# Expert features in three groups instead of six, with longer weight rows and small jobs between the products

## The chip, the cores and the metric

One core of one Trainium2 chip runs the whole program. The metric is device time in microseconds of one execution; before the change the median of three runs is 2388.02 us. Profiled executions come from the hardware profiler of the same core.

## What is computed

Two transformer blocks of depth 2 on 256 tokens of 1024 features, all in float32: the first with gated feed-forwards and a mixer, the second with a mixer per layer, a dense gated feed-forward in layer 0 and a mixture of experts in layer 1. The change touches the mixture of experts alone:

```python
def swiglu_2(h, w1, w3, w2):
    return (jax.nn.silu(h @ w1) * (h @ w3)) @ w2

def moe_swiglu(h, router_w, w1, w3, w2):
    logits = (h @ router_w).astype(jnp.float32)
    top_v, top_i = lax.top_k(logits, TOP_K)            # 2 of 8 experts
    ...
    for e in range(N_EXPERTS):
        y = y + gates[..., e:e + 1] * swiglu_2(h, w1[e], w3[e], w2[e])
    return y
```

Each expert has w1 and w3 of 1024 x 2816 and w2 of 2816 x 1024, 34.6 MB together; all eight are read, 277 MB.

## The kernel before

Every product is made exact in float32 from three products of a rounded type: a matrix is written as a high part (fp32r) plus a low part. For weights, `weights` (from L136) loads 1 MB into one of five buffers `raw` (the load is issued by SP, L143), then in two parts of 128 x 1024 elements ScalarE (ACT) makes the high part `whi` (L154) and VectorE (DVE) the low part `wlo` (L156). The pools `whi` and `wlo` hold eight parts each. `mm3` (L173 to L175) issues the three products of one operand pair: token high part with `whi`, token high part with `wlo`, token low part with `whi`. With 512 columns in each product a part of 128 x 1024 feeds six products.

The mixture of experts is the function `experts`. For each expert, at most 128 of its tokens are gathered (L1230, once for two experts), and the 2816 features are worked off in six groups: five of 512 and one of 256.

- Up products: x w1 and x w3 of a group go to a PSUM tile each (`mm`). Of 512 columns of w1 or w3, half the rows (512 rows, in DRAM runs of 2 KB) come with one load; the last group loads 1024 rows of 256 columns (runs of 1 KB).
- `hid`: ACT computes silu of the first (L1351), DVE multiplies it by the second (L1352).
- `flip` (L1261): TensorE (PE) transposes the group's `hid` in blocks of 128 into PSUM; ACT copies it as a high part (L179), DVE subtracts for the low part (L180).
- `down`: products with w2 (loads of 256 rows of 4 KB), added up in two PSUM tiles `acc` over all of the expert's groups.

In the program text these are a pipeline of three steps: after a group's up products come the `down` of two groups ago and the `flip` of one group ago. At an expert's end `scatter` splits the two output tiles, and the next expert's first group is followed by `add`, all of it at once: four products that put the slots back to their tokens (L1310) and four gated additions on DVE (L1315). The last expert's output meets the gate row first (L1291, L1307).

The order of instructions on each engine is set by a scheduler when the program is built; engines then run their own list in order, and wait where an input is missing. So where a waiting instruction stands in the list decides what stands behind it.

```python
                hid = self.s2([128, 512])[:, :n]
                nc.scalar.activation(hid, ps[0], AF.Silu)
                nc.vector.tensor_mul(hid, hid, ps[1])
                if stage2:
                    down(*stage2)
                stage2 = flip(*stage1) if stage1 else None
                stage1 = (e, f0, n, hid)
```

PSUM has four `mm` and four `acc` tiles of one bank each. A second round for experts with more than 128 tokens stands in a conditional block and is not run with these inputs.

Of the kernel before, what the change touches and what calls it, by code (L numbers as in the profile page):

```python
# [17 lines left out]
F32 = mybir.dt.float32  # L18
# [17 lines left out]
# parts of the first expert that are loaded to memory that later experts' tokens take: first feature, weights, half  # L36
EARLY = ((1024, "moe_w3_2", 1), (1536, "moe_w3_2", 1), (2048, "moe_w3_2", 1))
# [7 lines left out]
class Split:  # L45
    """A float32 matrix as the exact sum of two float32r parts, row block by row block."""
# [10 lines left out]
class Features:  # L57
    """x^T of both token tiles as the exact sum of two float32r parts; tiles [128, 2 token tiles, 4 blocks, 128]."""
# [14 lines left out]
class Kernel:  # L73
# [45 lines left out]
    def spare(self, src, nparts=2):  # L119
        """src: DRAM access [128, A, B]; loaded to 4 KB slots, in parts along A"""  # L120
# [7 lines left out]
    def behind(self):  # L128
        """Queues splits of weights behind an instruction of self.order = (instruction, splits that need not wait)"""
        if not self.order:  # L130
            return nullcontext()
        ins, free = self.order
        self.order = (ins, free - 1)
        return nullcontext() if free > 0 else self.tc.issue_after(ins)

    def weights(self, src, nparts=2, xs=None):  # L136
        """src: DRAM access [128, A, B]; its exact split, in parts along A. xs: the parts, if they are loaded already."""
# [8 lines left out]
        for x in xs:  # L146
# [3 lines left out]
            # in smaller steps where other work should find its place between them  # L150
# [9 lines left out]
    def columns(self, w, c0, n, k0=0, k1=None):  # L160
        """columns c0..c0+n of a [K, N] matrix as [128, K/128, n]"""
# [31 lines left out]
    def split_features(self, part, k0, k1, src):  # L193
        """src [128, k1 - k0, 256 tokens] -> blocks k0..k1 of a part"""
# [4 lines left out]
    def transpose_tile(self, X, t, x):  # L199
        """x: [128 tokens, features] of token tile t -> its part of X"""  # L200
# [14 lines left out]
    def feat(self, w, c0, X, n=512):  # L215
        """(x w)^T for n columns of w from c0: psum tiles [128 features, 2 blocks, 256 tokens]"""
# [56 lines left out]
    def rstd(self, ms, eps, n=1):  # L273
        """(ms + eps) ** -0.5 for [128, n]"""
# [8 lines left out]
    def constants(self):  # L283
# [16 lines left out]
        # 1 for the rows of the modulation that hold scale, 8..15 and 32..39  # L300
# [12 lines left out]
        # masks of the pairs (s, t): s on partitions, t along the free axis  # L313
# [22 lines left out]
        # vectors of parameters, one column per 128 of them  # L336
# [14 lines left out]
        # silu(c)  # L351
# [3 lines left out]
        # lower bounds of the first block's gates  # L355
# [19 lines left out]
        # 8 softplus(-lambda): max(-lam, 0) + log1p(exp(-|lam|)), the logarithm as 2 atanh(e / (2 + e))  # L375
# [25 lines left out]
    def plan_ada(self):  # L401
# [4 lines left out]
        for l in range(DEPTH):  # L406
# [4 lines left out]
            # what is loaded is used some time later  # L411
# [33 lines left out]
    def ada_load(self, l, st):  # L445
        """c w as rows [48, 128]; b, and b + 1 for scale; norm gain for scale, 1 elsewhere"""
# [9 lines left out]
    def ada_rows(self, l, st):  # L456
        """c w + b with norm gain * (1 + scale) in place of scale, to DRAM, to be read by every partition"""
# [11 lines left out]
    def hidden(self, pa, pb, out):  # L469
        """silu(pa) * pb -> out (float32)"""  # L470
# [4 lines left out]
    def ffn(self, X, w1, w3, w2, finish, ahead=None):  # L475
        """(silu(x w1) * (x w3)) w2; finish(t, psum halves of [128 tokens, 512]) once token tile t is complete"""
# [33 lines left out]
        # the first 512 features one token tile after the other, so that they can start on the first tile alone  # L510
# [60 lines left out]
    def head_out(self, o, gate):  # L571
        """o: psum [128 tokens, 512] of four heads -> rms-normalised per head, times gate [128, 512]"""
# [15 lines left out]
    def mixer1(self, l, X, finish):  # L588
# [23 lines left out]
        # the scores advance by one level with every tile of weights from here on  # L612
# [21 lines left out]
        # second branch, gated  # L634
# [49 lines left out]
    def project(self, Y, w, finish, order=((0,), (1,), (2, 3))):  # L684
        """Y w in steps of 256 rows of w, of which the last of the order go tile by tile"""
# [13 lines left out]
    def cumulate(self, lf, n):  # L699
        """running sums of lf [128, n * 64] within chunks of 64"""  # L700
# [27 lines left out]
    def hgrn_scores(self, qT, kT, lf):  # L728
        """sum_k q[t,k] exp(b[t,k] - b[s,k]) k[s,k] for s <= t. Pairs in the two halves of a block of 2n tokens take
# [791 lines left out]
```

## Time and profile before

| | |
|---|---|
| runs | 2388.02 us median of 3 (2386.01 to 2391.89) |
| profiled execution, first to last instruction (its span) | 2385.1 us; its own time is not listed apart from the span |
| PE busy | 2338.5 us, 98% |
| PE weight loads busy | 2073.4 us, 87% |
| DVE busy | 1849.2 us, 78% |
| ACT busy | 1421.7 us, 60% |
| mixture of experts | from about 1577 us to the end |
| DMA in the mixture of experts, 1600 to 2368 us | 342 GB/s |

How to read it: a matmul's end is modelled by the profiler and matmuls overlap, so that the busy time of PE says little of how much room it has; starts of matmuls are recorded, and the step from one start to the next shows a wait. The span lies 2.9 us under the median of the runs.

### The profile page before, as it was taken

To read this page: it belongs to the slowest core of one execution; us is meant where nothing else is said; L and a number is where in the kernel's file an instruction comes from. 1 tells how busy PE (TensorE), PEld (TensorE's weight loads), DVE (VectorE), ACT (ScalarE), POOL (GpSimd) and SP (SyncE) were. 2 spreads that over 40 slices of the span, in tenths; PEclk is the share of its full clock that TensorE was granted. 3 is DMA by queue.
4 is the path that set the end of the run, shared out by engine and by line. 5 is a ranking of instruction groups with operands and counts; after the bars stand their busy time and mean duration, and the time that the engine had idled before them with its cause. 6 is when DMAs were issued, how large, how long until landed. Compare 5 with 4: busy or idle time off the path is not lost.

```text
span 2385.1 us, 36351 instructions
## 1 busy us (share of the span) xinstructions
PE 2338.5 (98%) x14424; PEld 2073.4 (87%) x14424; DVE 1849.2 (78%) x2465; ACT 1421.7 (60%) x1960; POOL 64.2 (3%) x102
## 2 busy tenths in 40 slices
PE   8999999999999999999999999999999999999998
PEld 8998999999999999999788998878888887888876
DVE  6877877777786886764777556789988898898897
ACT  5444754454544664454475444778877777777775
POOL 0000000000000000000100001000000000000000
PEclk9999999999999999999999999999999999999999
DMA  8886446776788455575536555378999999999995
GB/s 284 300 326 205 141 163 201 261 259 232 265 311 289 152 168 185 193 246 189 182 108 221 184 188 198 107 280 321 356 337 334 350 345 343 357 338 353 367 346 215
DMA packets 277122, 608.07 MB, mean 255 GB/s; under 512 B 12976, under 2 KB 61630, under 8 KB 276944
## 3 DMA queue, kind: packets, MB, share of 16 engines
q1 hardware_dynamic: 269776, 590.52, 70.3%
q10 hardware_dynamic: 5696, 14.34, 2.0%
q8 instruction: 115, 1.88, 0.3%
q0 software_dynamic: 1472, 0.81, 0.1%
q14 instruction: 63, 0.52, 0.1%
HBM read 604.48 MB, written 1.15 MB: 254 GB/s over the span
## 4 chain that ended last, share of the span: by engine, by line
PE 89%; DVE 6%; ACT 2%; issue 2%; DMA 0%; POOL 0%; SPq 0%; POOLq 0%; ACTq 0%; DVEq 0%
PE mm L174 19%; PE mm L173 19%; PE mm L175 19%; PE acc L174 9%; PE acc L175 8%; PE acc L173 8%; DVE wlo L156 3%; ACT whi L154 1%; PE acc L775 1%; PE mm L1261 1%; PE mm L205 1%; PE mm L1230 1%; DVE s L180 0%; PE mm L1310 0%; PE mm L961 0%
## 5 line engine op out<-in xcount | busy, mean ns | idle before, releaser
L156 DVE TENSOR_TENSOR wlo<-raw,whi 128x1024 fp32r<-128x1024 f32 (+1 forms) x1302 | 1228.2, 986 | 349.3 <-ACT whi L154 344.8
L154 ACT ACTIVATE whi<-raw 128x1024 fp32r<-128x1024 f32 (+1 forms) x1302 | 1056.3, 865 | 549.3 <-PE mm L174 195.6
L173 PE MATMUL mm<-s,whi 128*128 128x256 f32 x2224 | 630.4, 284 | 2.6 <-ACT s L179 2.4
L175 PE MATMUL mm<-s,wlo 128*128 128x256 f32 x2224 | 629.3, 283 | 0.0
L174 PE MATMUL mm<-s,whi 128*128 128x256 f32 x2224 | 629.1, 283 | 0.0
L173 PEld LDWEIGHTS mm<-s,whi 128*128 128x128 f32 x2224 | 424.8, 191 | 6.5 <-ACT s L179 2.9
L174 PEld LDWEIGHTS mm<-s,whi 128*128 128x128 f32 x2224 | 425.1, 191 | 1.7
L175 PEld LDWEIGHTS mm<-s,wlo 128*128 128x128 f32 x2224 | 425.1, 191 | 0.5
L174 PE MATMUL mm<-wlo,s 128*128 128x512 f32 (+1 forms) x1184 | 421.7, 357 | 3.0 <-DVE wlo L156 2.2
L173 PE MATMUL mm<-whi,s 128*128 128x512 f32 (+1 forms) x1184 | 419.4, 354 | 3.5 <-ACT s L179 3.2
L175 PE MATMUL mm<-whi,s 128*128 128x512 f32 (+1 forms) x1184 | 415.4, 352 | 0.8 <-DVE s L180 0.8
L174 PE MATMUL acc<-wlo,s 128*128 128x512 f32 x984 | 387.9, 395 | 1.5
L175 PE MATMUL acc<-whi,s 128*128 128x512 f32 x984 | 383.4, 392 | 0.0
L173 PE MATMUL acc<-whi,s 128*128 128x512 f32 x984 | 376.7, 393 | 5.4 <-ACT s L179 5.4
L174 PEld LDWEIGHTS mm<-wlo,s 128*128 128x128 f32 x1184 | 226.0, 191 | 41.4 <-DVE wlo L156 13.7
L173 PEld LDWEIGHTS mm<-whi,s 128*128 128x128 f32 x1184 | 226.1, 191 | 35.5 <-ACT s L179 5.8
L175 PEld LDWEIGHTS mm<-whi,s 128*128 128x128 f32 x1184 | 225.6, 191 | 29.7 <-DVE s L180 1.8
L174 PEld LDWEIGHTS acc<-wlo,s 128*128 128x128 f32 x984 | 185.6, 189 | 46.4 <-DVE wlo L156 9.8
L173 PEld LDWEIGHTS acc<-whi,s 128*128 128x128 f32 x984 | 185.5, 189 | 44.4 <-ACT s L179 7.3
L175 PEld LDWEIGHTS acc<-whi,s 128*128 128x128 f32 x984 | 185.6, 189 | 38.7 <-DVE s L180 0.5
L179 ACT ACTIVATE s<-mm 128x512 fp32r<-128x512 f32 (+1 forms) x112 | 58.5, 540 | 90.8 <-PE mm L1261 55.7
L431 DVE SCALAR_TENSOR_TENSOR s<-raw,cact,s 128x1024 f32<-128x1024 f32 x84 | 107.3, 1278 | 0.6 <-DMA raw<-in_ada_w_dram 0.2
(308 smaller groups left out, 1374.8 us busy)
## 6 DMA issues: line engine op xcount, KB each, us to landing
raw<-in_moe_w_dram SPq DMA_DIRECT2D x261, 1024.0 KB, 6.1
raw<-in_ffn_w_dram SPq DMA_DIRECT2D x164, 1024.0 KB, 5.5
raw<-in_w_in_dram SPq DMA_DIRECT2D x60, 1024.0 KB, 5.2
raw<-in_ada_w_dram SPq DMA_DIRECT2D x48, 1024.0 KB, 7.0
raw<-in_w_out_dram SPq DMA_DIRECT2D x16, 1024.0 KB, 5.0
s<-rows ACTq DMA_DIRECT2D x10, 512.0 KB, 5.0
raw<-in_w_branch_b_dram SPq DMA_DIRECT2D x4, 1024.0 KB
raw<-in_w_branch_a_dram SPq DMA_DIRECT2D x4, 1024.0 KB
```

The lines of the kernel that those rows point to most:

```text
L154: nc.scalar.activation(h[:, c], x[:, c], AF.Copy)
L156: nc.vector.tensor_sub(l[:, c], x[:, c], h.bitcast(F32)[:, c])
L173: nc.tensor.matmul(out, lh, rh, start=start, stop=False, skip_group_check=skip)
L174: nc.tensor.matmul(out, lh, rl, start=False, stop=False, skip_group_check=skip)
L175: nc.tensor.matmul(out, ll, rh, start=False, stop=stop, skip_group_check=skip)
L179: nc.scalar.activation(h, src, AF.Copy)
L205: nc.tensor.transpose(p[:, j, :], x[:, (4 * q + j) * 128:(4 * q + j + 1) * 128], self.ident)
L431: nc.vector.scalar_tensor_tensor(acc, r[:, j, :], c, acc, op0=OP.mult, op1=OP.add)
L775: nc.tensor.matmul(p[:, h], d[:, h, c], q, start=True, stop=True)
L1230: nc.tensor.matmul(p[:, j, :], part[:, k * 128:(k + 1) * 128], S[ep][:, t], start=n == 0, stop=n == 3)
L1261: nc.tensor.transpose(p[:, j, :], hid[:, j * 128:(j + 1) * 128], self.ident)
```

## The change

Groups are now 1024, 1024 and 768 features. A load of w1 or w3 takes 256 rows of a group's whole width (runs of 4 KB, or 3 KB in the last group: 768 KB per load); a load of w2 takes for each partition two neighbouring rows, one run of 8 KB, and `flip` therefore transposes every second column of `hid`. A group has two PSUM tiles per weight matrix, of 512 and 512 (or 256) columns, and two `hid` tiles, with two silus in a row and two multiplications in a row. `flip`, gather, `back` and `add` use PSUM tiles of `acc` instead of `mm`. The pipeline has two steps: `down` of a group follows the up products of the next one, and its two flips stand between these products; gather steps, additions, output splits and `back` become jobs of which one is taken after every 256 rows of an up product. Three loads for the first expert that are made early change their shape in the same way. The rest of the diff drops comments, and gives the second round 16 buffers instead of 10.

```diff
-EARLY = ((1024, "moe_w3_2", 1), (1536, "moe_w3_2", 1), (2048, "moe_w3_2", 1))
+EARLY = ((1024, "moe_w3_2", 1), (1024, "moe_w3_2", 3), (2048, "moe_w3_2", 1))
+GROUPS = ((0, 1024), (1024, 1024), (2048, 768))
...
-        groups = [(i * 512, 512) for i in range(5)] + [(2560, 256)]
-        def flip(e, f0, n, hid):
-            nb = n // 128
-            p = self.mm([128, 4, 128])
+        def flip(hid, i, to):
+            nb = hid[i].shape[1] // 128
+            v = hid[i].rearrange("p (b m j) -> p b j m", j=2, m=128)
+            p = self.acc([128, 4, 128])
             for j in range(nb):
-                nc.tensor.transpose(p[:, j, :], hid[:, j * 128:(j + 1) * 128], self.ident)
+                nc.tensor.transpose(p[:, j, :], v[:, j // 2, j % 2, :], self.ident)
...
             for r0 in range(0, n, 256):
-                W = self.wrows(a["moe_w2_2"][0][e], f0 + r0)
-                for hf in range(2):
-                    for j in range(2):
-                        b = r0 // 128 + j
+                w = a["moe_w2_2"][0][e][f0 + r0:f0 + r0 + 256, :]
+                W = self.weights(w.rearrange("(p k) f -> p k f", k=2))
+                h, l = hl[r0 // 512]
+                for j in range(2):
+                    b = r0 % 512 // 128 + j
+                    for hf in range(2):
                         self.mm3(out[e][hf], (h[:, b, :], l[:, b, :]), W(j, hf * 512, (hf + 1) * 512),
...
-                for name in ("moe_w1_2", "moe_w3_2"):
-                    w = a[name][0][e]
-                    p = self.mm([128, 512])[:, :n]
...
-                hid = self.s2([128, 512])[:, :n]
-                nc.scalar.activation(hid, ps[0], AF.Silu)
-                nc.vector.tensor_mul(hid, hid, ps[1])
-                if stage2:
-                    down(*stage2)
-                stage2 = flip(*stage1) if stage1 else None
-                stage1 = (e, f0, n, hid)
+                widths = ((0, 512), (512, n - 512))
+                flips, to = [], {}
+                if prev:
+                    flips = [lambda i=i, hid=prev[3], to=to: flip(hid, i, to) for i in range(len(prev[3]))]
+                hid = []
+                for name in ("moe_w1_2", "moe_w3_2"):
+                    ps = [self.mm([128, 512])[:, :m] for _, m in widths]
+                    for kq in range(4):
+                        W = self.wcols(a[name][0][e], f0, n, kq * 256, kq * 256 + 256, ahead.get((e, f0, name, kq)))
+                        for k in range(2):
+                            for p, (b, m) in zip(ps, widths):
+                                self.mm3(p, X(2 * kq + k, c0, c0 + 128), W(k, b, b + m), kq + k == 0,
+                                         kq == 3 and k == 1)
+                        if flips and (hid or kq == 3):
+                            flips.pop(0)()
+                        else:
+                            step()
+                    if not hid:
+                        for p, (b, m) in zip(ps, widths):
+                            hid.append(self.s2([128, 512])[:, :m])
+                            nc.scalar.activation(hid[-1], p, AF.Silu)
+                    else:
+                        for h, p in zip(hid, ps):
+                            nc.vector.tensor_mul(h, h, p)
+                if prev:
+                    down(*prev[:3], to)
+                prev = e, f0, n, hid
```

Up to the first gather of the mixture of experts the lists of all engines are the same before and after; the number of products stays the same throughout. From there on the lists differ. Three places, as the program is built:

DVE at the end of a group's up products, before the change; L1352 is the multiplication that ends `hid`, `wlo_19822` and `wlo_19826` are the two low parts of the first load of w2 behind it.

```order
L156 TENSOR_TENSOR wlo_19801<-raw_19794,whi_19800 128x1024
L156 TENSOR_TENSOR wlo_19822<-raw_19819,whi_19821 128x1024
L1352 TENSOR_TENSOR s2_19816<-s2_19816,mm_19771 128x512
L156 TENSOR_TENSOR wlo_19826<-raw_19819,whi_19825 128x1024
L156 TENSOR_TENSOR wlo_19844<-raw_19841,whi_19843 128x1024
```

DVE at the end of an expert's first group, after the change; L1384 are the two multiplications, `wlo_19124` and `wlo_19128` the two low parts of the first load of w2.

```order
L158 TENSOR_TENSOR wlo_19100<-raw_19097,whi_19099 128x1024
L158 TENSOR_TENSOR wlo_19104<-raw_19097,whi_19103 128x1024
L1384 TENSOR_TENSOR s2_19004<-s2_19004,mm_19008 128x512
L1384 TENSOR_TENSOR s2_19006<-s2_19006,mm_19009 128x512
L158 TENSOR_TENSOR wlo_19124<-raw_19121,whi_19123 128x1024
L158 TENSOR_TENSOR wlo_19128<-raw_19121,whi_19127 128x1024
```

Before, one low part of w2 stands ahead of one multiplication; now none stands ahead of two.

PE at the same end before the change, from the last three products of the up tile (`mm_19771`) to the first product that takes the low part behind the multiplication (`wlo_19826`).

```order
L173 MATMUL mm_19771<-whi_19800,s4_18954 128x512
L174 MATMUL mm_19771<-wlo_19801,s4_18954 128x512
L175 MATMUL mm_19771<-whi_19800,s4_18955 128x512
L173 MATMUL acc_19211<-whi_19821,s2_19722 128x512
L173 MATMUL acc_19212<-whi_19821,s2_19722 128x512
L174 MATMUL acc_19211<-wlo_19822,s2_19722 128x512
L175 MATMUL acc_19211<-whi_19821,s2_19723 128x512
L173 MATMUL acc_19211<-whi_19825,s2_19722 128x512
L174 MATMUL acc_19212<-wlo_19822,s2_19722 128x512
L175 MATMUL acc_19212<-whi_19821,s2_19723 128x512
L173 MATMUL acc_19212<-whi_19825,s2_19722 128x512
L174 MATMUL acc_19211<-wlo_19826,s2_19722 128x512
```

PE at the end of the first group after the change; `mm_19008` and `mm_19009` are the two up tiles.

```order
L176 MATMUL mm_19008<-wlo_19104,s4_17033 128x512
L177 MATMUL mm_19008<-whi_19103,s4_17034 128x512
L176 MATMUL mm_19009<-wlo_19104,s4_17033 128x512
L177 MATMUL mm_19009<-whi_19103,s4_17034 128x512
L175 MATMUL acc_18472<-whi_19123,s2_19000 128x512
L175 MATMUL acc_18473<-whi_19123,s2_19000 128x512
L176 MATMUL acc_18472<-wlo_19124,s2_19000 128x512
L177 MATMUL acc_18472<-whi_19123,s2_19001 128x512
```

Eight products stood between the last up product and the first one that takes a low part from behind the multiplication. Now two products of the down step do, or four counted from the end of the first up tile.

PE at the end of an expert's second group after the change; L1267 are the transposes of the two `hid` tiles that the multiplications have just ended.

```order
L177 MATMUL mm_18363<-whi_18454,s4_17034 128x512
L176 MATMUL mm_18364<-wlo_18455,s4_17033 128x512
L177 MATMUL mm_18364<-whi_18454,s4_17034 128x512
L175 MATMUL acc_18472<-whi_18476,s2_18355 128x512
L175 MATMUL acc_18473<-whi_18476,s2_18355 128x512
L1267 MATMUL acc_18652<-ident_80,s2_18359 128x128 x4
L1267 MATMUL acc_18689<-ident_80,s2_18361 128x128 x4
L176 MATMUL acc_18472<-wlo_18477,s2_18355 128x512
```

The flips that the program text puts between the next group's products stand here right behind the group itself, ahead of the low products of w2.

## Rows read from the trace of the kernel before

**Rows 1.** The page: span, then busy time, share and instructions by engine.
```profile
span 2385.1 us, 36351 instructions
PE 2338.5 (98%) x14424; PEld 2073.4 (87%) x14424; DVE 1849.2 (78%) x2465; ACT 1421.7 (60%) x1960; POOL 64.2 (3%) x102
```
**Rows 2.** Stretches: PE, PEld, DVE, ACT, POOL busy (instructions), clock, DMA share, GB/s.
```profile
1600.00:1700.00 100.00, 100.00 (x483) 83.99 (x482) 92.95 (x104) 82.48 (x90) 0.00 (x0) 1.00 0.95 340
1700.00:1800.00 100.00, 100.00 (x489) 84.33 (x488) 87.30 (x87) 76.16 (x92) 0.00 (x0) 1.00 0.95 342
...
2200.00:2300.00 100.00, 99.31 (x459) 79.76 (x458) 88.78 (x87) 71.53 (x83) 0.00 (x0) 1.00 1.00 364
```
**Rows 3.** Waits, 1560 to 2385 us: us in total, times, longest.
```profile
DVE s L1352 <- PE mm L175: 20.5, 32, 1.5
...
PEld mm L174 <- DVE wlo L156: 13.7, 32, 1.0
...
PEld acc L174 <- DVE wlo L156: 9.8, 22, 0.5
...
ACT whi L154 <- DMA raw<-in_moe_w_dram: 4.2, 6, 1.0
```
**Rows 4.** Timeline at the end of one group: start, us, engine, line [idle before].
```profile
2192.38 0.39 PE L174 MATMUL mm<-wlo,s 128*128 128x512 f32 x1
...
2192.60 0.39 PE L175 MATMUL mm<-whi,s 128*128 128x512 f32 x1
...
2193.03 0.69 DVE L1352 TENSOR_TENSOR s<-s,mm 128x512 f32<-128x512 f32 x1 [0.86 <-PE mm L175]
...
2193.63 3.49 DVE L156 TENSOR_TENSOR wlo<-raw,whi 128x1024 fp32r<-128x1024 f32 x3
...
2194.41 0.39 PE L173 MATMUL acc<-whi,s 128*128 128x512 f32 x1
...
2194.91 0.50 PE L174 MATMUL acc<-wlo,s 128*128 128x512 f32 x1
...
2195.24 0.39 PE L175 MATMUL acc<-whi,s 128*128 128x512 f32 x1
2195.25 0.19 PEld L174 LDWEIGHTS acc<-wlo,s 128*128 128x128 f32 x1
2195.47 0.40 PE L174 MATMUL acc<-wlo,s 128*128 128x512 f32 x1
```
**Rows 5.** Timeline of DVE, the instructions next on it.
```profile
2197.04 0.68 DVE L180 TENSOR_TENSOR s<-acc,s 128x512 fp32r<-128x512 f32 x1
2197.64 1.21 DVE L156 TENSOR_TENSOR wlo<-raw,whi 128x1024 fp32r<-128x1024 f32 x1
```
**Rows 6.** Timeline of PE: three transposes of a flip.
```profile
1910.09 0.49 PE L1261 MATMUL mm<-ident,s 128*128 128x128 f32 x3
```
**Rows 7.** Groups of instructions by form, 1550 to 2385 us: count, busy, mean ns, idle.
```profile
L156 DVE TENSOR_TENSOR wlo<-raw,whi 128x1024 fp32r<-128x1024 f32 x523 | 610.0, 1218 | 42.1 <-ACT whi L154 41.4
...
L1261 PEld LDWEIGHTS mm<-ident,s 128*128 128x128 f32 x176 | 22.2, 140 | 6.0
...
L1352 DVE TENSOR_TENSOR s<-s,mm 128x256 f32<-128x256 f32 x8 | 3.3, 417 | 2.7 <-PE mm L175 2.7
```
**Rows 8.** Timeline of ACT: a silu, a copy for a flip, two high parts.
```profile
2169.45 0.60 ACT L1351 ACTIVATE s<-mm 128x512 f32<-128x512 f32 x1 [4.07 <-PE mm L175]
2169.94 0.38 ACT L179 ACTIVATE s<-mm 128x256 fp32r<-128x256 f32 x1
2170.21 2.01 ACT L154 ACTIVATE whi<-raw 128x1024 fp32r<-128x1024 f32 x2
```
**Rows 9.** DMA, 1560 to 2385 us: GB/s in 40 slices, and the loads of expert weights.
```profile
GB/s 225 286 347 323 321 348 365 341 353 340 333 306 354 325 376 360 318 334 343 362 341 315 359 365 359 356 313 363 325 355 361 355 383 353 368 361 320 351 256 55
...
raw<-in_moe_w_dram SPq DMA_DIRECT2D x255, 1024.0 KB, 6.1
```

More of the change, by code (lines that the diff above doesn't have):

```diff
@@ L1201, in experts @@
             for f0, name, kh in EARLY:
-                ahead[0, f0, name, kh] = self.spare(self.columns(a[name][0][0], f0, 512, kh * 512, kh * 512 + 512))
+                ahead[0, f0, name, kh] = self.spare(self.columns(a[name][0][0], f0, dict(GROUPS)[f0], kh * 256, kh * 256 + 256))
         if rnd:
@@ L1298, in scatter, with part @@
-            return lambda: add(e, parts, direct)
-        def add(e, parts, direct):
-            for t in range(2):
-                for hf in range(2):
-                    c = slice(hf * 512, (hf + 1) * 512)
-                    p = self.mm([128, 512])
-                    st = ST[e // 2][:, e % 2, t]
+                parts = []
+                def part(hf=hf, parts=parts):
+                    y = out[e][hf]
                     if direct:
-                        nc.tensor.matmul(p, st.bitcast(F32), parts[hf][0], start=True, stop=True)
-                    else:
-                        for i in range(2):
-                            nc.tensor.matmul(p, st, parts[hf][i], start=i == 0, stop=i == 1)
-                    if e == 0 and not direct:
-                        nc.vector.tensor_scalar(ysum[t][:, c], p, gates[t][:, e:e + 1], None, op0=OP.mult)
-                        continue
-                    y = (x if direct else ysum)[t][:, c]
-                    nc.vector.scalar_tensor_tensor(y, p, gates[t][:, e:e + 1], y, op0=OP.mult, op1=OP.add)
-                    if e == NE - 2 and not direct:
-                        merge.append(lambda t=t, c=c, y=y: (nc.vector.tensor_mul(y, y, row[0][:, c]),
-                                                            nc.vector.tensor_add(x[t][:, c], x[t][:, c], y)))
-                if e == NE - 1:
-                    store(t, x[t], row[1])
@@ new lines, in part @@
+                        y = self.s2([128, 512]) if rnd else self.s4([128, 512])
+                        nc.vector.tensor_mul(y, out[e][hf], row[0][:, hf * 512:(hf + 1) * 512])
+                        parts.append(y)
+                    else:
+                        yh = self.s2([128, 512], F32R)
+                        yl = self.s2([128, 512], F32R)
+                        self.split_to(yh, yl, y)
+                        parts.extend((yh, yl))
+                if hf == 0 or direct:
+                    part()
+                else:
+                    jobs.append(part)
@@ new lines, in scatter, with add @@
+                for t in range(2):
+                    jobs.append(lambda t=t, hf=hf, parts=parts: add(e, t, hf, parts, direct))
+        def add(e, t, hf, parts, direct):
+            c = slice(hf * 512, (hf + 1) * 512)
+            p = self.acc([128, 512])
+            st = ST[e // 2][:, e % 2, t]
+            if direct:
+                nc.tensor.matmul(p, st.bitcast(F32), parts[0], start=True, stop=True)
+            else:
+                for i in range(2):
+                    nc.tensor.matmul(p, st, parts[i], start=i == 0, stop=i == 1)
+            if e == 0 and not direct:
+                nc.vector.tensor_scalar(ysum[t][:, c], p, gates[t][:, e:e + 1], None, op0=OP.mult)
+                return
+            y = (x if direct else ysum)[t][:, c]
+            nc.vector.scalar_tensor_tensor(y, p, gates[t][:, e:e + 1], y, op0=OP.mult, op1=OP.add)
+            if e == NE - 2 and not direct:
+                jobs.append(lambda: (nc.vector.tensor_mul(y, y, row[0][:, c]),
+                                     nc.vector.tensor_add(x[t][:, c], x[t][:, c], y)))
+            if e == NE - 1 and hf:
+                store(t, x[t], row[1])
@@ L1326, in experts, with finish @@
             then[0]()
[L1327 to L1328 removed]
+        for s in steps:
+            s()
+        prev = None
+        def finish():
+            hid, to = prev[3], {}
+            for i in range(len(hid)):
+                flip(hid, i, to)
+            down(*prev[:3], to)
         for e in range(NE):
             c0 = (e % 2) * 128
[L1331 to L1356 removed]
@@ L1357, in experts @@
+            for f0, n in GROUPS:
+                if f0 == 0 and e % 2 == 0:
+                    jobs.append(lambda e=e: back(e // 2))
+                elif f0 == 0 and e + 1 < NE:
+                    Y, steps = gather((e + 1) // 2)
+                    jobs.extend(steps)
+                elif e == NE - 2 and not row:
+                    row.append(self.modrow(layer, 5))
+                    row.append(self.bcast(a["final_g_2"], 0, D))
                 if (e, f0) == (0, 2048) and then:
                     then[1]()
-                if e % 2 == 0:
-                    if f0 == 0:
-                        back(e // 2)
-                elif e + 1 < NE:
-                    if f0 == 0:
-                        Y, steps = gather((e + 1) // 2)
-                    elif steps:
-                        steps.pop(0)()
+                widths = ((0, 512), (512, n - 512))
[13 more added lines that the diff above has]
+                            flips.pop(0)()
+                        else:
+                            step()
[3 more added lines that the diff above has]
+                            nc.scalar.activation(hid[-1], p, AF.Silu)
+                    else:
+                        for h, p in zip(hid, ps):
+                            nc.vector.tensor_mul(h, h, p)
+                if prev:
+                    down(*prev[:3], to)
+                prev = e, f0, n, hid
@@ L1367, in experts @@
             if e % 2:
                 X = Y
-        down(*stage2)
-        down(*flip(*stage1))
-        late.pop()()
+        finish()
+        while jobs:
+            step()
     def moe(self, l, x, hs, lg, sel, place, rest, store):
```

50 lines of the change are left out of this document (10 added, 40 removed).

## The prediction

> **What bounds the kernel now.** I read the page first, then the stretches, then the waits, then one piece of the timeline. By the page PE is busy 98% of 2385.1 us, DVE 78%, ACT 60% [rows 1]. Busy time of overlapping matmuls proves little, so the reader should look at instructions per stretch. From 1600 to 1800 us, early in the experts, PE starts 483 and 489 matmuls per 100 us at full clock with no idle time, DVE being busy 93% and 87% and DMA 95% [rows 2]. Between 2192.38 and 2194.41 us nine products of 512 columns start, 0.226 us each [rows 4]; nothing there waits, so 0.226 us is what a product costs.
>
> The number of products does not change, so only PE's waits can. The waits name one releaser, the low parts that DVE makes: 13.7 us in 32 waits and 9.8 us in 22 [rows 3]. They are idle time of weight loads. What a wait costs the products is seen at one group's end [rows 4]: the last up product starts at 2192.60; the multiplication, which needs it, starts 0.43 us later, at 2193.03; the split behind it at 2193.63, a step of 0.60; the product that takes this low part starts at 2194.91, another 1.28. That chain is 2.31 us. PE had nine products to do, 2.03 us, so it waits 0.28. The product behind it then comes 0.33 us later instead of 0.226: a restart costs 0.10 more. With 54 waits of this size, 54 x 0.37 = 20 us are all that the change can win back on PE in the experts.
>
> Loads do not bound: ACT waits for weights 4.2 us in all [rows 3], while a 1 MB load lands 6.1 us after its issue [rows 9] and five buffers are there.
>
> By the Trainium skill (Perfetto Trace Analysis, Identifying the Most-Contended Engine) PE's room is judged by the busy share of its weight loads. That share is 80% between 2200 and 2300 us [rows 2], which by the rule leaves a fifth of the time as room; the steps of 0.226 us without a wait say that there is none, and I go by these.
>
> **The seam of a group, the main term.** DVE works its list in order. Before, one low part of w2 stood ahead of one multiplication, and eight products filled PE's time to the next low part. After, two multiplications stand ahead of the first low part. At the same prices the chain from the last product of the first up tile is 0.43 + 2 x 0.60 + 1.28 = 2.91 us [rows 4].
> - First group of an expert: PE has that product, two more up products and two of `down`, 5 x 0.226 = 1.13. Wait 1.78, in the last five experts. In the third expert multiplications and splits alternate: 2.31 against six products (1.36) is 0.95, the second split adds 0.28, together 1.2.
> - Second group: the same five products and eight transposes. Three transposes start and end within 0.49 us with 0.27 for the last (its mean) [rows 6], so a step is 0.11 and eight are 0.88. Wait 2.91 - 2.01 = 0.90, five times; once a gather stands between and fills it.
> - Third group: the second multiplication has 256 columns, 417 ns against about 685 for 512 [rows 4, 7], so the chain is some 0.27 shorter, 2.64. PE's list holds about 1.7 us there. Wait 0.95, four times; twice a gather fills it.
>
> Sum: 5 x 1.78 + 1.2 + 5 x 0.90 + 4 x 0.95 = 18.4 us. In the first two experts the list has DVE several loads ahead at every seam (over 5 us of products), so no wait. Before, 16 seams have the eight products and pay 0.28: 4.5 us. **Term: +13.9 us.** It goes straight onto the time, since PE has nothing else in its list.
>
> **The silu in the middle of a group.** ACT too works in order. In both lists two high parts stand ahead of the silu. A silu takes a step of 0.49, a 512-wide copy for a flip about as much, two high parts 2.01 together, so one is ready about 1.0 later, and DVE adds its 1.28 [rows 8, 4]. After, the chain of two silus, a copy and a split is 0.43 + 0.49 + 0.49 + 0.27 to 0.49 + 1.1 + 1.28 = 4.1 to 4.3 us, against some 3.7 to 3.9 us of products: 0.2 to 0.6 at ten places, about 4 us, and nine places of 0.17 where a flip's copy alone delays a high part, 1.5. Before, one silu and a copy leave 0.1 to 0.4 at 21 places, 3.8 us. Term: +2 us; from 0, if ACT's idle time absorbs it, to +6, if the waits are each as long as the longest.
>
> **Restarts.** About 40 waits by the count instead of 54, at 0.10: -1.4 us.
>
> **Costed at nothing.** (1) Per expert 16 splits of 768 columns take the place of 12 of 1024. The step for 1024 is (2197.04 - 2193.63) / 3 = 1.14, for 512 columns 0.60 [rows 4, 5]; between them 0.87, so 13.9 us against 13.7. It lies in DVE's idle 11% [rows 2]; uncovered it is 2 us over all experts. (2) Longer rows of the loads: at most the 4.2 us that ACT waits [rows 3] can be won. The other way, in the last group 768 KB are used up in two parts of 3 x 0.226 + 3 x about 0.12 us, 2.08 us, that is 378 GB/s, where the slices show 383 at most [rows 9]. It lasts for eight loads, 17 us, and the buffers cover a shortfall; if DMA stayed at the stretch's 341 GB/s, 1.8 us per expert are late, up to 14 in all. (3) Transposes of every second column: the trace has no strided weight load. 176 of 140 ns each [rows 7]; lower end 0, upper end the step of 0.11 doubled, 19 us. I take 0, because only bytes between the elements change, and keep the upper end. By the Trainium skill (SBUF — State Buffer, Door 1: The DMA port swizzle) float32 reads may skip within a 16-byte line at full rate, which gives 0; no run here shows it. (4) Flips, gathers and additions in `acc` tiles: two of the four hold an expert's output, and the output is read before the next pair is needed, so I find no wait; one would cost a split, 1.14. (5) Start and end: same list up to the first gather, same four last products and gated additions.
>
> **Sum.** 13.9 + 2 - 1.4 = 14.5 us. The profiled span 2385.1 becomes 2399.6. The median of the runs lies 2.9 above that span, so the forecast is 2402 us, 0.6% slower.
>
> **The rivals.**
> - *Waits fall instead.* Gathers, additions and output splits no longer come in one bunch. In the old list these, and not the seams, follow the longest waits (1.0 us, [rows 3]); if DVE then reaches each seam late by its own work, and the two multiplications find their products done, half or all of the 20 us goes: 2368 to 2378. It decides if DVE does not idle ahead of L1384. Against it: DVE waited ahead of L1352 32 times before, 20.5 us [rows 3], and the list puts nothing behind which it could be late. Chance 0.11. The share rule above, with its fifth of room, would shorten 768 us of experts down to DVE's 89%, some 85 us, to 2303: 0.02, as the steps speak against it.
> - *No difference.* 24 seams take the place of 48. Of the 20 us, 4.5 + 3.8 and 5.4 of restarts are explained; about 6 are left. If these vanish by the finer jobs, and the term for the silu is 0, and one in five seams is hidden behind a gather that I count as too early, +14.5 becomes +3 to +7: 2391 to 2395. Chance 0.27.
> - *Much slower.* Strided transposes cost their 19 us, or the 3 KB loads starve ACT, up to 14: 2416 to 2421. For it: DMA is at 95% to 100% [rows 2]. Against it: hardly a wait for a load. Chance 0.08.
> - *The change does not do what it says.* In part that is so: the flips stand in the list not between the next group's products but at the group's end, the reason for the forecast's waits of 0.90; it has no chance of its own.
>
> **How the numbers follow.** Forecast 2402, chance 0.52, own range 2396 to 2412 (silu term 0 to +6, some seams more or less). A run of this kernel is told from no change at about 0.3%, 7 us, so faster is below 2381, slower above 2395. Faster 0.13, same 0.27, slower 0.52 + 0.08 = 0.60. The range 2380 to 2415 leaves out most of the first rival and most of the third, about 0.19.
>
> **What would show it.** In the profile after: matmul steps still 0.226 without a wait; 768-wide splits near 0.87 in step; DVE waiting for PE ahead of L1384 about 20 times; and PE's waits for low parts fewer and longer, about 25 us in all and up to 1.8 each, at `down` products behind the first group, and flips waiting for L1384 behind the second. ACT's waits for loads stay under 5 us. Wrong is the forecast if the seams show gaps below 0.5 us, if transposes step by 0.2, or if ACT waits for loads by tens of microseconds.

## The result, and the profile after

The kernel after took 2404.17 us (median of 4 runs, 2400.85 to 2405.02), the kernel before beside it 2387.2 us (4 runs, 2386.01 to 2391.89). The ratio is 1.0064, with a 95% interval of 1.0052 to 1.0076: slower by 0.6%, with 2402 forecast. The profiled execution has a span of 2402.4 us and a time of 2404.14 us.

The page after, as [rows 1] before:

```profile
span 2402.4 us, 36533 instructions
...
PE 2342.2 (97%) x14424; PEld 2080.7 (87%) x14424; DVE 1851.9 (77%) x2497; ACT 1426.9 (59%) x1992; POOL 64.1 (3%) x102
```

Busy times hardly move: DVE has 2.7 us more work in a span 17.3 us longer. The stretches of [rows 2], in the same columns:

```profile
1600.00:1700.00 100.00, 100.00 (x491) 84.50 (x490) 93.66 (x110) 85.29 (x101) 0.00 (x0) 1.00 0.91 328
1700.00:1800.00 100.00, 99.14 (x469) 82.46 (x468) 85.32 (x87) 70.92 (x84) 0.00 (x0) 1.00 0.91 338
2200.00:2300.00 100.00, 97.12 (x450) 79.48 (x450) 86.60 (x89) 70.96 (x85) 0.00 (x0) 1.00 0.95 358
```

Early in the experts PE still hardly idles, and the granted clock is full in all three stretches; from the third expert on it idles, and 2200 to 2300 us holds 450 matmuls in place of 459. The waits (us in all, times, longest), as [rows 3], with the multiplication on L1384 now:

```profile
DVE s L1384 <- PE mm L177: 25.2, 17, 2.0
ACT whi L156 <- DMA raw<-in_moe_w_dram: 20.8, 26, 1.8
...
PEld acc L176 <- DVE wlo L158: 16.9, 21, 2.0
...
PEld mm L176 <- DVE wlo L158: 12.3, 27, 1.0
PE acc L176 <- DVE wlo L158: 10.8, 11, 1.6
PEld acc L1267 <- DVE s L1384: 4.1, 9, 0.6
```

What grew are the waits of the `down` products (acc) for low parts and of the transposes (L1267) for the multiplication; the waits in the middle of a group (mm) stayed. One seam of a first group, the timeline of PE and DVE:

```profile
2197.91 0.39 PE L177 MATMUL mm<-whi,s 128*128 128x512 f32 x1
...
2198.34 1.28 DVE L1384 TENSOR_TENSOR s<-s,mm 128x512 f32<-128x512 f32 x2 [1.97 <-PE mm L177]
...
2198.59 0.61 PE L175 MATMUL acc<-whi,s 128*128 128x512 f32 x2
...
2199.54 2.35 DVE L158 TENSOR_TENSOR wlo<-raw,whi 128x1024 fp32r<-128x1024 f32 x2
...
2200.82 0.50 PE L176 MATMUL acc<-wlo,s 128*128 128x512 f32 x1 [1.61 <-DVE wlo L158]
```

The chain runs from 2197.91 to 2200.82, 2.91 us, with two multiplications ahead of the low part. The second of the two products of 2198.59 starts at 2198.82, and the next product 2.00 us later; less a step of 0.227 that is 1.77 us of wait ([rows 4] had 0.28). PE does so at five seams; at the first seam of the third expert it waits 0.95 and, one split later, 0.24.

To follow all of PE's losses I add up, over the trace from 1600 us to the last product with weights, what the steps between starts of matmuls have beyond 0.227 us (512 columns), 0.12 (256) or 0.108 (transposes), where this is over 0.06 us. With it the 17.3 us divide as follows (rounded), all from the two traces:

| us | before | after | difference |
|---|---|---|---|
| losses at `down` products and transposes (the seams) | 8.1 | 21.3 | +13.2 |
| losses at up products (the middle of a group) | 12.7 | 10.8 | -1.9 |
| other losses | 0.6 | 0.5 | -0.1 |
| other steps, from the first router product (`h @ router_w`, at 1563 us) to the last product with weights | 785.5 | 788.7 | +3.2 |
| from there to the end of DVE's last instruction | 9.9 | 10.1 | +0.3 |
| from there to the end of the span | 5.6 | 7.4 | +1.8 |
| start of the first router product | 1562.8 | 1563.5 | +0.7 |

Nothing ahead of the experts was edited, so the last row is scatter of single profiles. The row above it is not. DVE's last instructions, before and after:

```profile
2378.12 1.42 DVE L1408 SCALAR_TENSOR_TENSOR s<-s,t,s 128x512 f32<-128x512 f32 x2 [0.73 <-POOL t L279]
```

```profile
2393.58 1.42 DVE L1429 SCALAR_TENSOR_TENSOR s<-s,t,s 128x512 f32<-128x512 f32 x2 [0.73 <-POOL t L281]
```

The spans end 5.6 and 7.4 us behind them. That time is 5.5 to 5.6 us in the profiles of all three versions built on the kernel before, and 7.4 to 7.8 in all eleven built on the kernel after, so the change brought about 1.8 us there. In that time SP stands still for 1.8 to 2.3 us between two instructions that only wait for semaphores, where the versions on the kernel before have no gap over 0.5 us. Why it does so is open; no run varied it.

### The profile page after: what moved, and what is told of

It is laid out like the page before. It is cut to its first block, busy times and chain, and to the rows that moved or that the text cites. A ratio compares the mean times of both kernels' runs of the same rounds, so it can differ in the third digit from the quotient of the medians.

```text
span 2402.4 us, 36533 instructions
## 1 busy us (share of the span) xinstructions
PE 2342.2 (97%) x14424; PEld 2080.7 (87%) x14424; DVE 1851.9 (77%) x2497; ACT 1426.9 (59%) x1992; POOL 64.1 (3%) x102
## 4 chain that ended last, share of the span: by engine, by line
PE 91%; DVE 5%; ACT 2%; issue 1%; POOL 0%; DMA 0%; SPq 0%; POOLq 0%; ACTq 0%; DVEq 0%
PE mm L176 19%; PE mm L175 19%; PE mm L177 19%; PE acc L176 9%; PE acc L177 9%; PE acc L175 9%; DVE wlo L158 2%; PE acc L777 1%; PE acc L1232 1%; PE mm L207 1%; PE acc L1267 1%; ACT whi L156 1%; PE acc L1321 0%; DVE s L1384 0%; ACT s L181 0%
## 5 line engine op out<-in xcount | busy, mean ns | idle before, releaser
L158 DVE TENSOR_TENSOR wlo<-raw,whi 128x1024 fp32r<-128x1024 f32 (+2 forms) x1334 | 1230.0, 967 | 331.5 <-ACT whi L156 327.7
L156 ACT ACTIVATE whi<-raw 128x1024 fp32r<-128x1024 f32 (+2 forms) x1334 | 1059.9, 851 | 575.4 <-PE mm L176 197.2
L177 PE MATMUL mm<-whi,s 128*128 128x512 f32 (+1 forms) x1184 | 414.1, 352 | 0.8 <-DVE s L182 0.8
L176 PE MATMUL acc<-wlo,s 128*128 128x512 f32 x984 | 388.0, 394 | 10.9 <-DVE wlo L158 10.8
L175 PE MATMUL mm<-whi,s 128*128 128x512 f32 (+1 forms) x1184 | 392.6, 355 | 2.8 <-ACT s L181 2.6
L175 PEld LDWEIGHTS mm<-whi,s 128*128 128x128 f32 x1184 | 223.9, 191 | 33.4 <-ACT s L181 5.2
L176 PEld LDWEIGHTS acc<-wlo,s 128*128 128x128 f32 x984 | 185.7, 189 | 54.0 <-DVE wlo L158 16.9
L181 ACT ACTIVATE s<-s 128x512 fp32r<-128x512 f32 (+2 forms) x85 | 50.3, 624 | 79.1 <-DVE s L475 51.0
```

Of the source, the lines that this page charges most:

```text
L156: nc.scalar.activation(h[:, c], x[:, c], AF.Copy)
L158: nc.vector.tensor_sub(l[:, c], x[:, c], h.bitcast(F32)[:, c])
L175: nc.tensor.matmul(out, lh, rh, start=start, stop=False, skip_group_check=skip)
L176: nc.tensor.matmul(out, lh, rl, start=False, stop=False, skip_group_check=skip)
L177: nc.tensor.matmul(out, ll, rh, start=False, stop=stop, skip_group_check=skip)
L181: nc.scalar.activation(h, src, AF.Copy)
```

## The experiments

All ratios are to the kernel before beside it, with a 95% interval; 0.1 points (0.001 of the ratio) are 2.4 us. PE's losses are counted as above.

**Both multiplications behind the first low parts.** The load and split of the first 256 rows of w2 are taken out of `down` and called ahead of the multiplications, which are queued behind its last low part (`self.last`, kept by `weights`):

```
+                        first = rows(*prev[:2], 0) if prev else None
+                        with self.tc.issue_after(self.last) if prev else nullcontext():
-                        for h, p in zip(hid, ps):
-                            nc.vector.tensor_mul(h, h, p)
+                            for h, p in zip(hid, ps):
+                                nc.vector.tensor_mul(h, h, p)
...
-                    down(*prev[:3], to)
+                    down(*prev[:3], to, first)
```

> Theory (order at the seams: both multiplications stand ahead of the first low part of w2, so DVE's chain 0.43 + 2 x 0.60 + 1.28 outlasts PE's list): with the two low parts of the first w2 load ahead of the multiplications the products of `down` find their low parts done. The waits of 1.77 us at five first groups and of about 0.6 at second and third groups go, 12 to 16 us in all: 2388 to 2393 us. PE's and PEld's waits for wlo at acc products fall from about 28 us to under 10. Rival A (loads: 768 KB groups and ACT's 20.8 us of waits for DMA set the time): the loads are as they were, what is won at the seams is lost again at the next split, 2401 to 2407. Rival B (transposes with a strided weight load set it): the same, 2401 to 2407.

Measured: 2388.06 us, ratio 0.9998 (0.9989 to 1.0007), 0.66 points under the kernel after: 15.8 us, uncertain by some 4 us by the two intervals. The seam's timeline, with the multiplication on L1389:

```profile
2187.49 0.39 PE L177 MATMUL mm<-whi,s 128*128 128x512 f32 x1
...
2187.68 1.28 DVE L1389 TENSOR_TENSOR s<-s,mm 128x512 f32<-128x512 f32 x2
...
2187.71 0.61 PE L175 MATMUL acc<-whi,s 128*128 128x512 f32 x2
2188.16 0.39 PE L176 MATMUL acc<-wlo,s 128*128 128x512 f32 x1
```

PE goes through the seam at steps of 0.226. The waits for low parts at acc products are 2.3 and 0.5 us (16.9 and 10.8 after), PE's losses 14.5 us in place of 32.6. The loads are as in the kernel after and ACT still waits 15.1 us for them, so that rival falls, and the transposes' with it. The theory holds.

**One low part's load between the multiplications.** The same, but only the second multiplication is queued behind the low parts (`issue_after(self.last) if prev and i else nullcontext()`, i being the number of the multiplication).

> Half the dose of e1_rows_ahead: the low parts of the first w2 load stand between the two multiplications, not ahead of both. Theory: the chain is 0.60 us shorter than in the kernel after (2.31 in place of 2.91 us), so the wait at a first group is 1.77 - 0.60 = 1.2 us; 0.4 to 0.6 us less at each of 14 seams, 6 to 8 us: 2395 to 2399 us. Rival (it is the place of the flips or the loads, not the length of this chain): as after, 2402 to 2406, or all of it, 2386 to 2390.

Measured: 2401.25 us, ratio 1.0052 (1.0038 to 1.0065). The size was wrong, the place not:

```profile
2197.64 0.69 DVE L1389 TENSOR_TENSOR s<-s,mm 128x512 f32<-128x512 f32 x1 [2.00 <-PE mm L177]
...
2197.89 0.61 PE L175 MATMUL acc<-whi,s 128*128 128x512 f32 x2
...
2199.51 0.50 PE L176 MATMUL acc<-wlo,s 128*128 128x512 f32 x1 [1.01 <-DVE wlo L158]
```

The wait at a first group is 1.17 us by the steps, 0.60 shorter as expected, five times, 3.0 us; the time fell by 2.9, though the two intervals overlap, and PE's losses by 2.6 (to 30.0). At second groups the order of PE's list changed with it: four transposes in place of eight stand ahead of the product that waits, and it waits 0.57 as in the kernel after (0.56). At third groups PE's list has a transpose right behind the last up product, and that waits for the first multiplication, which this edit leaves where it was. So by the lists the seams of second and third groups hang on the transposes' place as well as on the low part's; when both multiplications moved, the transposes moved behind more `down` products too. No run moved the transposes alone at a seam.

**Rows of 4 KB and transposes of columns side by side, in the kernel after**

```
-            v = hid[i].rearrange("p (b m j) -> p b j m", j=2, m=128)
-                nc.tensor.transpose(p[:, j, :], v[:, j // 2, j % 2, :], self.ident)
+                nc.tensor.transpose(p[:, j, :], hid[i][:, j * 128:(j + 1) * 128], self.ident)
...
-                W = self.weights(w.rearrange("(p k) f -> p k f", k=2))
+                W = self.wrows(a["moe_w2_2"][0][e], f0 + r0)
```

> The kernel after, but with w2 in rows of 4 KB and flips that transpose columns side by side, as before. Theory (order at the seams): the seams stay, only the transposes' step goes from 0.120 back to 0.108 us, 176 x 0.012 = 2 us: 2400 to 2403 us. Rival A (loads): rows of 8 KB land no faster than rows of 4 KB would if it is wrong; if it is right that rows matter, ACT waits longer, 2405 to 2412. Rival B (strided weight loads of 205 ns in place of 140): the steps of the flips sum to 6.6 us more than before, and more where a weight load is waited for: 2390 to 2398.

Measured: 2402.98 us, ratio 1.006 (1.0046 to 1.0075). **The same edit the other way, in the kernel before:**

> The kernel before with this part of the change alone: w2 in rows of 8 KB, flips that transpose every second column. Theory (order at the seams): seams as before, transposes 176 x 0.012 = 2 us dearer, weight loads of 205 ns: 2388 to 2391 us against 2387. Rival A (loads): longer rows take away ACT's 4.2 us of waits for loads, 2382 to 2386. Rival B (strided weight loads): 2393 to 2405.

Measured: 2391.13 us, ratio 1.0007 (0.9997 to 1.0017). The first is 1.0 us under the kernel after, the second 1.7 us over the kernel before; both agree with a cost of 1 to 2 us, and neither excludes 0. ACT's waits for loads hardly change (19.4 us for 20.8 after, 4.3 for 4.2 before). Rows and transposes change together here, so no time shows either alone. The transposes' weight loads by form (count, busy, mean ns), in the kernel after and, below, with columns side by side:

```profile
L1267 PEld LDWEIGHTS acc<-ident,s 128*128 128x128 f32 x176 | 26.4, 205 | 6.3 <-DVE s L1384 4.1
```

```profile
L1266 PEld LDWEIGHTS acc<-ident,s 128*128 128x128 f32 x176 | 20.6, 140 | 8.1 <-DVE s L1382 4.9 <-DVE s L1324 0.2
```

A load of every second column takes 205 ns in place of 140, but on PE's path only the step of a transpose counts, 0.120 in place of 0.109 us at its median between two transposes in these two kernels; all 176 steps sum to 18.1 us with it in the kernel before, 17.1 without.

**Loads of w1 and w3 in halves.** Two transfers of half the columns into the same buffer.

```
-            nc.sync.dma_start(r, src)
+            for c in halves or (slice(0, B),):
+                nc.sync.dma_start(r[:, :, c], src[:, :, c])
```

> The kernel after with each load of w1 and w3 in two transfers of half the columns, rows of 2 KB (and 1 KB in the last group) in place of 4 KB (3 KB). Theory (order at the seams): loads are hidden, 2401 to 2408 us, the last half of a load landing 6 to 8 us after its issue. Rival A (loads set the time): shorter rows and twice as many issues take bandwidth, ACT waits for loads over 40 us in all in place of 20.8, and the time goes to 2412 to 2440.

Measured: 2404.89 us, ratio 1.007 (1.0056 to 1.0084), no difference from the kernel after. ACT's wait grew as the rival had it only in part, and cost nothing:

```profile
ACT whi L157 <- DMA raw<-in_moe_w_dram: 27.1, 33, 2.4
```

**The remedy in the kernel before.** Two low parts ahead of its one multiplication, in place of one (`down` takes the first split as an argument, the multiplication is queued behind it).

> The kernel before with the same remedy: the low parts of the first w2 load ahead of the multiplication (two in place of one). Theory: the waits of 0.28 us and their restarts at some 16 seams go, 3 to 6 us: 2382 to 2386 us; the groups' size costs nothing by itself. Rival (smaller groups bound by something else: silus, additions, gathers in a bunch): 2386 to 2391 us.

Measured: 2383.34 us, ratio 0.9972 (0.996 to 0.9985). The waits at acc products fall from 9.8 us [rows 3] to 3.3, PE's losses from 21.4 to 18.2 us: 5.3 less at the seams and 2.2 more in the middle of groups. So the kernel before paid for its seams too, and with the remedy it is 0.26 points, some 6 us, ahead of the kernel after with it, uncertain by some 4 us. Only 3 of these us have a place in the two profiles: 2.1 at the end of the program, 0.3 in the last additions and 0.6 in the experts themselves.

**The middle of a group.** The first try was to queue the silus on ACT behind the next load's high parts, on top of the remedy:

```
+                        if hid and kq == 0:
+                            with self.tc.issue_after(self.high):
+                                for h, p in zip(hid, up):
+                                    nc.scalar.activation(h, p, AF.Silu)
```

> The kernel e1_rows_ahead, and the two silus of a group queued on ACT behind the high parts of the next load of weights. Theory: the eight waits of 0.5 to 0.75 us in the middle of a group (4.7 us in all in the profile of e1_rows_ahead) come from ACT idling ahead of the silus while high parts stand behind them; they go, 2382 to 2385 us. Rival (ACT's order does not matter, as another wait takes their place: the copy of a flip comes later): 2386 to 2390 us.

Measured: 2387.85 us, ratio 0.999 (0.9981 to 0.9999): a miss, but not a test of the theory, since the edit changed nothing. In the two profiles the instructions of PE, ACT and DVE come in the same order from the first to the last; two high parts stood ahead of the silus already. ACT without the edit and, below, with it:

```profile
2038.52 1.58 ACT L156 ACTIVATE whi<-raw 128x768 fp32r<-128x768 f32 x2 [1.60 <-DMA raw<-in_moe_w_dram]
2042.93 0.87 ACT L1384 ACTIVATE s<-mm 128x512 f32<-128x512 f32 x2 [2.83 <-PE mm L177]
2043.69 0.61 ACT L181 ACTIVATE s<-acc 128x512 fp32r<-128x512 f32 x1
2044.17 4.52 ACT L156 ACTIVATE whi<-raw 128x768 fp32r<-128x768 f32 x6
```

```profile
2043.43 0.87 ACT L1375 ACTIVATE s<-mm 128x512 f32<-128x512 f32 x2 [2.81 <-PE mm L177]
2044.19 0.61 ACT L181 ACTIVATE s<-acc 128x512 fp32r<-128x512 f32 x1
2044.67 3.06 ACT L156 ACTIVATE whi<-raw 128x768 fp32r<-128x768 f32 x4
```

It idles 2.8 us, then does both silus and a flip's copy, and the high parts follow at once, without a wait for a load. PE's wait there, one of eight of 0.53 to 0.74 us by the steps in both profiles (PE's losses are 14.5 us in both):

```profile
2046.63 0.50 PE L176 MATMUL mm<-wlo,s 128*128 128x512 f32 x1 [0.44 <-DVE wlo L158]
```

So what the next expectations draw from it, that it moved none of the waits, has no weight. The run is of use as a measure of scatter: the same order was measured at 0.9998 and at 0.999, 2 us apart. The same with rows of 4 KB, transposes side by side and the last additions in the order of before:

> The kernel e5_silu_behind with w2 in rows of 4 KB and flips of columns side by side, and the last additions in the order of before (first token tile, then second). Theory: against e5_silu_behind 1 to 2 us less for the weight loads of the transposes and 0.3 us less at the end: 2380 to 2384 us. Rival (rows of 8 KB were of use, the silus are no bound): 2386 to 2392 us.

Measured: 2383.55 us, ratio 0.9976 (0.9966 to 0.9986). Of the 4 us 1 to 2 were expected, and the profile shows as much: the experts are 1.4 us shorter and the last additions 0.3. No row shows the others, and PE's losses are not smaller (15.1 us).

Then the flips were moved one load earlier (`kq >= 2` in place of `kq == 3`), on that kernel and, alone, in the kernel after:

> The kernel e7_best with both flips placed behind the third and fourth load of the first product of a group in place of the fourth and fifth, so that their copies stand ahead of the silus on ACT. Theory (new, after e5_silu_behind moved none of the eight waits in the middle of a group: DVE's low part of a flip stands ahead of the splits, waits for ACT's copy, and that stood behind the silus): the eight waits of 0.53 to 0.84 us go, 4 to 5 us: 2378 to 2381 us. Rival (the waits come from ACT's late high parts or from loads): they stay, 2382 to 2386 us.

> The kernel after with the flips' place alone changed in the same way; multiplications still stand ahead of the first low part. Theory: the waits in the middle of a group go, 4 to 5 us, the waits of 1.77 us at five first groups stay: 2397 to 2401 us. Rival (both kinds of wait are one, DVE's list as a whole being too long): 2402 to 2406 us, as what is won there is lost at the seams.

Measured: 2387.87 us, 1.0001 (0.9992 to 1.001), and 2406.91 us, 1.0077 (1.0064 to 1.0091): both misses. The second does not differ clearly from the kernel after (1.0064). The copies are out of the way, but the jobs in their old place (a gather's or an addition's) now stand there, and PE loses 18.4 us in the first of the two, 15.1 without the edit. Next, the copy alone went to DVE:

> The kernel e7_best with the high part of each group's second flip copied on DVE in place of ACT. Theory for the waits in the middle of a group (after e5_silu_behind and e9_best_early): ACT's own list is the chain, 0.43 + two silus 0.87 + copy 0.49 + high part, and only then DVE's low part; without the copy on ACT the high parts come 0.49 us sooner, the eight waits of 0.53 to 0.84 us shrink to 0.1 to 0.4, 2 to 4 us in all: 2379 to 2382 us against 2383.6. Rival (DVE's list is the chain: it has 0.6 us more to do there; or loads that come late keep ACT from working ahead): the waits stay or grow, 2383 to 2388 us.

Measured: 2383.67 us, 0.998 (0.997 to 0.9991): the rival's time. At the place shown above the wait went, and one of 0.29 us stands six products later; new ones of 0.48 us stand behind additions, and PE's losses stayed (15.3 us). Shortening what stands behind the silus moved the waits. The last run lets ACT work ahead instead: the silus wait for four high parts, not two (`kq == 1` in place of `kq == 0` in the edit above).

> The kernel e7_best with the two silus behind the high parts of the second, not the first, load of the next product, so that four high parts are made in the 2.8 us for which ACT idles ahead of them. Theory (the waits in the middle of a group come from ACT standing ahead of silus while high parts could be made): the waits of 0.53 to 0.84 us go at most of eight places, 3 to 5 us: 2378 to 2381 us against 2383.6. Rival (the loads are not there yet, ACT's 16 us of waits for DMA being their cause): ACT's waits for loads grow instead and the time stays, 2383 to 2387 us.

Measured: 2379.11 us, ratio 0.9957 (0.9944 to 0.997), the fastest version here. The waits of ACT (for loads; of silus for PE), first with two high parts ahead, then with four:

```profile
ACT s L1377 <- PE mm L177: 42.8, 17, 4.6
...
ACT whi L156 <- DMA raw<-in_moe_w_dram: 16.2, 19, 1.7
```

```profile
ACT whi L156 <- DMA raw<-in_moe_w_dram: 33.4, 49, 3.1
...
ACT s L1377 <- PE mm L177: 8.4, 10, 1.5
...
PEld mm L176 <- DVE wlo L158: 4.2, 12, 1.1
```

ACT's idle time ahead of silus fell by 34 us and its waits for loads doubled; PE's losses are 9.3 us in place of 15.1, with one of the eight waits in the middle of a group left (0.84 us, ahead of the product of 2192.11). Against the kernel without the edit that is 4.5 us, uncertain by some 4. What was missing was lead, not a shorter chain.

## Why the prediction was right, point by point

- **What bounds.** PE's steps of 0.226 us without a wait were taken as the floor and its waits as all that can change. The floor held; the waits were most of the change, but 1.8 us at the end of the program and some 3 us of small steps were not among them. By the Trainium skill (Perfetto Trace Analysis, Identifying the Most-Contended Engine) the weight loads' share would leave a fifth as room; that share is 79.48% from 2200 to 2300 us after (79.76 in [rows 2]), and the fastest version here stands at 0.9957 of the kernel before. The steps decided, not the share.
- **The seam, +13.9 us.** The mechanism and the size held. The chain of 2.91 us and the wait of 1.78 at five first groups were measured as 2.91 and 1.77, and 1.2 at the third expert as 0.95 and 0.24. At the second groups the chain is 2.90 us as forecast (2132.40 to 2135.30), and the wait comes in pieces, 0.56 ahead of the product and twice 0.11 among the transposes, 0.78 for a forecast of 0.90; the transposes' longer step takes the rest:

```profile
2132.40 0.39 PE L177 MATMUL mm<-whi,s 128*128 128x512 f32 x1
...
2133.57 1.35 PE L1267 MATMUL acc<-ident,s 128*128 128x128 f32 x8
2135.30 0.50 PE L176 MATMUL acc<-wlo,s 128*128 128x512 f32 x1 [0.39 <-DVE wlo L158]
```

  At the third groups it is 0.59 and 0.11, 0.70 for 0.95. With all restarts the losses at seams grew by 13.2 us, for 12.5 forecast with the term for restarts. By the time, undoing the order gave 15.8 us and the seams before were worth 6.7 (0.28 points); the difference, 9 us, is uncertain by some 5 us to both sides, so the time alone would not settle the size.
- **The silu, +2 us.** This term had the wrong sign. The side after was right: waits of 0.38 to 0.75 stand at nine places in the middle of a group, 4.9 us, for a forecast of 4 to 5.5. The side before was too low: 3.8 us were forecast, but the losses at up products were 12.7 us before and 10.8 after, 1.9 less, so here waits fell, as the first rival had it, perhaps by the finer jobs, which no run tested. The prediction also blamed the chain behind the silu; the runs show that too few high parts were made ahead of it, since the kernel with more lead on ACT gained 4.5 us (0.9976 to 0.9957).
- **Costed at nothing.** Longer rows: right in both kernels, loads of 1 MB land in 6.8 us (6.1 in [rows 9]). ACT's waits for loads were to stay under 5 us and came to 20.8. That was wrong, and it is one of the prediction's own signs of a wrong forecast (tens of microseconds); it was a poor sign, as the time shows no cost: 33.4 us of such waits go with the fastest version. Strided transposes: taken as 0, measured at 1.0 us by the steps, far from the 19 of the upper end. By the Trainium skill (SBUF — State Buffer, Door 1: The DMA port swizzle) reads go at full rate where consecutive ones fall into the same 16-byte line, as two reads of every second float32 column do; the weight loads of 205 ns in place of 140 do not agree with it. The splits of 768 columns have a mean of 954 ns where 0.87 us a step was worked out; a mean holds more than a step, and the steps agree:

```profile
2260.31 1.82 DVE L158 TENSOR_TENSOR wlo<-raw,whi 128x768 fp32r<-128x768 f32 x2
```

  Two in 1.82 us are a step of 0.87 and a last one of 0.95. Start and end were not equal: the order of the additions took 0.3 us and the program's end 1.8, a cost that the prediction didn't look for.
- **The sum.** From the first router product to the last product with weights the kernel after took 14.5 us more, the very sum of the forecast, but not by its terms: 13.2 at the seams, -1.9 in the middle of groups, and 3.2 in small steps, of which strided transposes explain about 1. Of the 1.8 us at the end 1.1 were hidden, because the forecast put the median 2.9 us above the span, and after the change it is 1.8 above it. So the forecast's 0.1% is better than its working deserves: one term was right, and the errors of the others cancelled.

## What to carry to other kernels

Where an engine works its list in order, look at what stands ahead of the first instruction that the next stage needs: two instructions of 0.6 us that wait for a stage's last result held PE up by as much as 1.77 us at a seam, some 16 us in all, and no busy share told of it. Put work that is ready ahead of work that must wait, and check by a wait's place, not by its sum. Compare the engines' order before and after an edit first: one run here changed the program's text, left the order as it was, and could teach nothing about the wait that it was made for. And where a wait moves when the chain behind it is shortened, give the engine ahead of it more lead instead, that is, more work done before it has to wait.

## What the runs showed of the hardware

A weight load of 128 float32 columns takes 140 ns from columns side by side and 205 ns from every second one; a transpose behind it steps by 0.120 instead of 0.109 us. Weights in rows of 2, 4 or 8 KB made no difference in time that could be measured at 328 to 358 GB/s (those of 8 KB together with the strided transposes), and an engine's waits for loads went from 16.2 to 33.4 us while the kernel became 4.5 us faster. The profiled executions start their experts at times up to 5 us apart from one version to another (the first product of the places between 1567.9 and 1573.0 us), though nothing ahead of them was edited, so a difference of 2 us between the spans of two single profiles says nothing here by itself.
